# A decoder layer on eight cores: seven-product V projection, a six-row ring in the down projection, and work moved between ScalarE, VectorE and GpSimd

## The chip, the cores and the metric

One Trainium2 chip, all eight cores (two dies: cores 0 to 3 and 4 to 7); each core computes 2048 of 16384 tokens. The metric is the device time of one execution in microseconds (us), that of the slowest core. Some executions of any kernel here fall into a slow state, in which the cores of a die run at a lower granted clock (3339.6 us with die 1 at 0.81 to 0.82, in one execution of the changed kernel; 2976.8 us in one of the kernel before).

Engines: PE is TensorE, DVE is VectorE, ACT is ScalarE, POOL is GpSimd, SP issues transfers.

## The reference, cut to what matters

```python
proj = x @ w_in + b_in                 # x (16384, 2048); columns: qa ka va | qb kb vb
# group A: 8 heads of 128, dilated causal attention, three patterns (window, dilation)
#          (128,1) (512,4) (2048,16), mixed by their softmax denominators
# group B: 16 query heads of 64, 2 key/value heads, sliding window of 128, sinks
# rope on q and k of both groups; RMSNorm of each group; concatenated, @ w_out
x = layer_norm(alpha * x + mixer(x))
x = layer_norm(alpha * x + (silu(x @ w_gate) * (x @ w_up)) @ w_down)      # D_FF = 5632
```

The values va have 1024 columns (A), vb has 128 (B).

## The kernel before

Rope is the rotation of queries and keys by position; PV is the product of the attention weights with V. A core goes through these stages: start (first load, V of token tiles t = 0 and 1), *projection stage* (K of t = 0, then for each tile of 512 tokens V and K, to the first query projection), *sliding-window stage* (32 units u of group B, with query projections in between), *dilated stage* (32 units of group A), out-projection, *MLP stage*, tail (last layer norm). The MLP stage already uses a seven-product (Strassen) scheme: in a down stage a pair p of output rows takes products "1" to "7" in banks BA to BD; `acc` (VectorE) adds a bank into rows `xq` of the residual, which came from memory (x1s in the first half g = 0, the unfinished z2s in the second, g = 1). There are four down stages: two halves of the tokens (st) by two halves of D_FF (g).

```python
# projection stage: V of a block of 128 tokens, plain; B columns in 384-wide groups
groups = [(0, 512), (512, 1024)] if (t < 4 and ...) else [(0, 384), (384, 768), (768, 1152)]
for kc in range(KC):
    matmul(bank(k, bk)[:, 0:c1 - c0], x[:, kc, blk*128:blk*128+128], wv[:, kc, c0:c1], ...)
# K of tile t, head h: 16 matmuls of 512, then a rope of four VectorE operations, then a 128 KB store
# ...
def a_banks(u):                                  # dilated stage: where unit u sums its output
    return (6, 7) if u >= 26 and u % 2 else (OB, LB)
# a unit: 3 scores -> exp on ScalarE -> mask product on VectorE -> PV in a_banks(u)
#         -> a_evac (VectorE reads the bank) -> a_square (ScalarE) -> sum of squares (GpSimd)
# ...
D_OFF = [WB + (24576, 13312, 0)[i] for i in (0, 1, 2, 0, 1, 2, 1, 0)]   # slots of down weights d0..d7
for p in range(8):                               # a down stage
    nxq = load_xq(p + 1)                         # rows of the next pair, five-row ring
    if p == 0:
        for i, bk in (("5", BB), ("2", BC), ("4", BA), ("1", BD)):
            P(i, bk, True, False, range(NJ - 1)) # all but the last h chunk
    ...                                          # the rest of 5, 2, 4, 1, then 3, 7, 6
```

The softmax here doesn't subtract the row's maximum and nothing guards it: scores larger than these inputs give would overflow.

## Time and profile before

| | us |
|---|---|
| executions | 2860.21, 2857.76 fast; 2917.7, 2976.8 slow |
| span of the cores in the profiled execution | 2846.2 to 2858.0, clock 0.99 |
| TensorE busy | 2754.1 (96%) |

Median of the eight cores for each stage, from the starts of the matmuls that open them:

| stage | before, us |
|---|---|
| start | 83.9 |
| projection stage | 417.6 |
| sliding-window stage | 205.7 |
| dilated stage, u = 0 to 25 | 202.1 |
| dilated stage, end: u = 26 to the out-projection | 31.9 |
| out-projection | 230.3 |
| MLP stage | 1649.6 |
| tail | 32.5 |

The lines that show what bounds each of them stand in the prediction. One view is added here, TensorE's timeline of core 7 at the end of the dilated stage; columns are start, duration, engine, line of the kernel, operation, output and input, shape, count, and in brackets the idle time ahead of it with what ended it.

```profile
914.68 0.99 PE L921 MATMUL sp<-arena 128*128 128x128 bf16 x8 [2.25 <-DVE arena L892]
923.98 0.65 PE L947 MATMUL sp<-arena 128*128 128x32 bf16 x17 [0.72 <-DVE arena L900]
929.05 0.65 PE L947 MATMUL sp<-arena 128*128 128x32 bf16 x17 [0.80 <-DVE arena L900]
```

L892 and L900 are VectorE's mask products. After one wait of 2.25 us each unit loses some 0.8 us; the periods of u = 26 to 30, from one unit's first PV matmul to the next, are 6.54, 5.72, 5.01, 5.07 and 5.07 us.

### The profile page before, as it was taken

The numbers are of one execution on the slowest core, as the hardware profiler recorded it, in microseconds if no ns is written. First come the engines' busy times: TensorE is split into PE (matmuls) and PEld (weight loads), VectorE is DVE, ScalarE is ACT, GpSimd is POOL, SyncE is SP. The second block draws the span as 40 slices with busy tenths as digits, with TensorE's granted clock in tenths as the row PEclk, the third lists the DMA queues.
The fourth block names the chain that finished last, engine by engine and source line by source line (L and its number), as shares of the span: only waits on it lengthen the run. The fifth ranks groups of instructions, "written<-read, shape, count | busy, mean of one in ns | idle before, by whom it ended". The sixth has DMA issues, their size and how long they took to land.

```text
span 2858.0 us, 41512 instructions; the slowest of 8 cores (2846.2 to 2858.0 us)
## 1 busy us (share of the span) xinstructions
PE 2754.1 (96%) x15081; PEld 1319.9 (46%) x15081; DVE 1933.6 (68%) x2707; ACT 736.6 (26%) x1078; POOL 562.8 (20%) x569
## 2 busy tenths in 40 slices
PE   6999999999999999999998999988999999999996
PEld 2445555444666444444443444433444444444442
DVE  0654555788788826788865666655888765666667
ACT  0000000576666327333200122111333200212115
POOL 4000000122111567411100000045200000000165
PEclk9999999999999999999999999999999999999998
DMA  9975213668666769799999755699788799555763
GB/s 156 183 138 111 62 52 87 114 98 134 152 138 167 215 144 239 140 151 151 148 159 184 138 89 87 96 199 200 155 175 172 123 196 175 103 89 89 148 133 118
DMA packets 250810, 400.58 MB, mean 140 GB/s; under 512 B 89072, under 2 KB 127088, under 8 KB 249840
## 3 DMA queue, kind: packets, MB, share of 16 engines
q0 software_dynamic: 94272, 186.43, 45.6%
q1 hardware_dynamic: 141936, 182.12, 23.5%
q10 hardware_dynamic: 14400, 29.37, 3.2%
q8 instruction: 122, 2.00, 0.3%
q14 instruction: 80, 0.66, 0.1%
HBM read 491.42 MB, written 97.06 MB: 206 GB/s over the span
## 4 chain that ended last, share of the span: by engine, by line
PE 84%; DMA 7%; DVE 3%; issue 3%; ACT 3%; POOL 1%; DVEq 0%; ACTq 0%; SPq 0%; POOLq 0%
PE sp L1399 49%; PE sp L494 8%; PE sp L1206 8%; PE sp L481 6%; PE sp L742 6%; DMA arena<-wdn 2%; DMA z2s<-arena 1%; DMA arena<-wv 1%; DMA arena<-x1s 1%; DMA arena<-z2s 1%; PE sp L550 1%; ACT arena L791 1%; DVE arena L1745 1%; POOL arena L140 1%; PE sp L514 1%
## 5 line engine op out<-in xcount | busy, mean ns | idle before, releaser
L1399 PE MATMUL sp<-arena 128*128 128x512 f16 x7408 | 1611.0, 380 | 35.7 <-DVE arena L1745 29.8
L1399 PEld LDWEIGHTS sp<-arena 128*128 128x128 f16 (+1 forms) x7408 | 725.3, 98 | 921.7 <-issue 58.0
L1662 DVE TENSOR_TENSOR arena<-sp,arena 128x512 f32<-128x512 f32 (+1 forms) x348 | 236.5, 688 | 160.7 <-PE sp L1399 145.3
L1745 DVE TENSOR_TENSOR arena<-arena,sp 128x512 f32<-128x512 f32 x257 | 167.8, 682 | 135.9 <-PE sp L1399 122.7
L742 PE MATMUL sp<-arena 128*128 128x512 bf16 x1024 | 237.0, 380 | 3.8 <-DVE arena L375 1.5
L1206 PE MATMUL sp<-arena 128*128 128x512 bf16 x1024 | 221.8, 379 | 1.0 <-DVE arena L1195 1.0
L494 PE MATMUL sp<-arena 128*128 128x512 bf16 x1024 | 222.2, 379 | 0.0
L140 POOL DMA_DIRECT2D arena<-wup x88 | 65.7, 747 | 782.1 <-DVE arena L1412 501.0
L463 DVE TENSOR_TENSOR arena<-sp,arena 128x384 bf16<-128x384 f32 (+1 forms) x81 | 48.1, 605 | 203.0 <-PE sp L481 120.0
L481 PE MATMUL sp<-arena 128*128 128x384 bf16 (+1 forms) x1040 | 182.6, 337 | 0.0
L1412 DVE TENSOR_TENSOR arena<-arena 128x2048 f16<-128x2048 bf16 (+1 forms) x118 | 158.9, 1347 | 30.7 <-DMA arena<-wdn 30.7
L1249 POOL TENSOR_TENSOR arena<-arena 128x512 f32<-128x512 f32 x117 | 150.3, 1285 | 145.1 <-DVE arena L1745 107.5
L1696 ACT ACTIVATE arena<-sp 128x512 f32<-128x512 f32 x86 | 51.4, 597 | 436.4 <-PE sp L1399 436.4
L1420 DVE TENSOR_TENSOR arena<-arena 128x2048 f16<-128x2048 bf16 (+1 forms) x118 | 159.3, 1350 | 0.0
L1251 POOL TENSOR_TENSOR arena<-arena 128x512 f32<-128x512 f32 x117 | 156.7, 1340 | 10.4 <-ACT arena L1248 8.0
L1206 PEld LDWEIGHTS sp<-arena 128*128 128x128 bf16 x1024 | 100.0, 98 | 122.9 <-issue 3.2
L1662 DVE TENSOR_TENSOR arena<-arena 128x512 f16<-128x512 f32 (+1 forms) x304 | 155.0, 568 | 2.4 <-DMA x1h<-arena 2.4
L494 PEld LDWEIGHTS sp<-arena 128*128 128x128 bf16 x1024 | 100.2, 98 | 120.3
L369 ACT ACTIVATE arena<-sp,arena 128x512 bf16<-128x512 f32 (+1 forms) x37 | 24.7, 666 | 506.1 <-PE sp L514 430.8
L1248 ACT ACTIVATE arena<-arena 128x512 f32<-128x512 f32 x117 | 73.7, 630 | 311.2 <-DVE arena L1745 160.4
L742 PEld LDWEIGHTS sp<-arena 128*128 128x128 bf16 x1024 | 95.9, 98 | 123.2 <-issue 14.8
L481 PEld LDWEIGHTS sp<-arena 128*128 128x128 bf16 x1040 | 101.7, 98 | 79.6
(145 smaller groups left out, 2493.1 us busy)
## 6 DMA issues: line engine op xcount, KB each, us to landing
arena<-wup POOLq DMA_DIRECT2D x88, 1024.0 KB, 10.8
arena<-wdn POOLq DMA_DIRECT2D x32, 1408.0 KB, 19.0
z2s<-arena SPq DMA_DIRECT2D x48, 512.0 KB, 11.9
arena<-wob SPq DMA_DIRECT2D x32, 512.0 KB, 7.2
arena<-xres SPq DMA_DIRECT2D x32, 512.0 KB, 8.7
x1s<-arena ACTq DMA_DIRECT2D x64, 256.0 KB, 8.8
arena<-x1s SPq DMA_DIRECT2D x32, 512.0 KB, 13.5
arena<-z2s SPq DMA_DIRECT2D x32, 512.0 KB, 15.6
```

The lines of the kernel that those rows point to most:

```text
L140: i = self._add(q, lambda: eng.dma_start(out=out, in_=in_), reads, writes, joins, semkey=semkey)
L481: ins = nc.tensor.matmul(bank(k, bk)[:, 0:c1 - c0], x[:, kc, blk * 128:blk * 128 + 128], wv[:, kc, c0:c1], start=(kc == 0), stop=(kc == KC ...
L494: ins = nc.tensor.matmul(bank(k, bk), wk[h][:, kc, :], x[:, kc, :], start=(kc == 0), stop=(kc == KC - 1))
L742: ins = nc.tensor.matmul(bank(k, bk), w[:, kc, :], x[:, kc, :], start=(kc == 0), stop=(kc == KC - 1))
L1206: ins = nc.tensor.matmul(bank(k, bk), w[:, kc, :], y[:, kc, hh * 512:(hh + 1) * 512], start=(first and i == 0), stop=(last and i == len(kc ...
L1249: S_.pool(lambda: nc.gpsimd.tensor_tensor(out=za, in0=za, in1=z, op=ALU.add), [bz, bza], [bza])
L1251: ss["pend"] = [lambda: S_.pool(lambda: nc.gpsimd.tensor_tensor(out=qa, in0=qa, in1=sq, op=ALU.add), [bsq, bqa], [bqa])]
L1399: ins = nc.tensor.matmul(bank(k, bk), w, x, start=(first and i == 0), stop=(last and i == len(ws) - 1), skip_group_check=True)
L1412: S_.dve(lambda: nc.vector.tensor_tensor(out=v, in0=w[:, 0:n, :], in1=w[:, n:2 * n, :], op=ALU.add), [bw], [b])
L1420: S_.dve(lambda: nc.vector.tensor_tensor(out=v, in0=w[:, :, 0:128], in1=w[:, :, 128:256], op=ALU.subtract), [bw], [b])
L1662: S_.dve(lambda: nc.vector.tensor_tensor(out=o, in0=a, in1=b, op=op), [ba, bb], [bo])
L1745: S_.dve(lambda: nc.vector.tensor_tensor(out=v, in0=v, in1=o, op=op), [b, bo], [b])
```

## The change

Its intent: fewer matmuls in V (a seven-product scheme for the 1024 A columns of t = 2 to 7), and no waits for weights and rows in the down stages. To find room for V's sums one of the five x slots is given up, and another holds two rope tables until x of t = 7 needs it. The rest moves small work from VectorE to ScalarE or from ScalarE to GpSimd. The core of the diff, with cuts:

```diff
+    if swap:                                   # rope_a: the half swap as two ScalarE copies, one VectorE product
+        for i, j in ((0, 64), (64, 0)):
+            S_.act(lambda i=i, j=j: nc.scalar.activation(out=t2[i:i + 64], in_=ps[j:j + 64], func=AF.Identity, ...
-    xs = [view(k, XO + i * X_SLOT, ...) for i in range(5)]
+    xs = [view(k, XO + i * X_SLOT, ...) for i in range(4)]
-    def v_tile(t, blk): ...
+    def w_sum(i): ...      # five sums of blocks of wv (128x4096), once
+    def x_sum(t, i): ...   # three sums of blocks of x for each tile
+    def v_unit(t, i, mid=None): ...   # products 4 5 1 2 3 7 6, eight matmuls of 512 each, for 256 tokens
+    def vb_tile(t): ...    # B columns: 64 matmuls of 128 columns
-    load_ra(0)
+    load_ta(0)
+    load_ta(1)             # second rope table, ahead of V of t = 1
 ...
-        return (6, 7) if u >= 26 and u % 2 else (OB, LB)
+        return (6, 7) if u >= 28 and u % 2 else (OB, LB)
 ...
-            S_.act(lambda: nc.scalar.activation(out=sq, in_=yc, func=AF.Square), [byc], [SQ[1]])
+            if 26 <= 4 * h + c < 31:
+                S_.pool(lambda: nc.gpsimd.tensor_tensor(out=sq, in0=yc, in1=yc, op=ALU.mult), [byc], [SQ[1]])
+            else:
+                S_.act(lambda: nc.scalar.activation(out=sq, in_=yc, func=AF.Square), [byc], [SQ[1]])
 ...                          # sliding-window stage: dilated q ropes one step later, three with swap on ScalarE;
                              # dilated stage: run(dveq, 2 if u < 27 else 4), before u < 26
-        proj(u + LEAD, mid=lambda: run(peq, 1))
         run(dveq, 4)
+        proj(u + LEAD, mid=(lambda: run(peq, 1)) if u < 31 else first_a)
 ...
-D_OFF = [WB + (24576, 13312, 0)[i] for i in (0, 1, 2, 0, 1, 2, 1, 0)]
+D_OFF = [WB + (13312, 24576, 0)[p % 3] for p in range(8)]
 ...                          # down stages: six-row ring, rows of pair p + 2 asked for in the middle of pair p
+                e = (3, 4, 5, 2, 0, 1)[n % 6]
-                nxq = load_xq(p + 1) if p < 7 else None
+                    if p < 6:
+                        load_xq(p + 2)
 ...                          # first pair: product 2 whole, ahead of the last h chunk
+                        P(i, bk, True, i == "2", None if i == "2" else range(NJ - 1))
 ...                          # x1h of the other half of the tokens: in halves, over seven pairs
-                    if 1 <= p <= 4:
-                        load_x1((B11, B22, B12, B21)[p - 1])
+                    for i in {6: (6, 7), 7: ()}.get(p, (p,)):
+                        load_x1(i)
```

## The prediction

> **What bounds the kernel now.** I read the list of cores first, then the page's first part. The eight cores lie within 2846 to 2858 us at a granted clock of 0.99, so any of them may stand for all; the third timed run (2917.7) is the slow state, and the fast time is 2859 (2857.8 and 2860.2).
>
> ```profile
> PE 2754.1 (96%) x15081; PEld 1319.9 (46%) x15081; DVE 1933.6 (68%) x2707; ACT 736.6 (26%) x1078; POOL 562.8 (20%) x569
> ```
>
> TensorE is busy for 96% of the span. So time can go in two ways only: fewer matmuls, or less of the 2858 - 2754 = 104 us in which TensorE idles. Some 22 us of that lie in the first load of x and wv, and 27 us behind the last matmuls (VectorE and ScalarE finish the layer norm there); the change touches neither. About 55 us are in reach. Next, the groups of instructions kept apart by shape, for what the matmuls cost:
>
> ```profile
> L494 PE MATMUL sp<-arena 128*128 128x512 bf16 x1024 | 222.2, 379 | 0.0
> L481 PE MATMUL sp<-arena 128*128 128x384 bf16 x816 | 134.1, 326 | 0.0
> L481 PE MATMUL sp<-arena 128*128 128x512 bf16 x224 | 48.7, 379 | 0.0
> L872 PE MATMUL sp<-arena 128*128 128x128 bf16 x256 | 21.5, 228 | 0.0
> L921 PE MATMUL sp<-arena 128*128 128x128 bf16 x256 | 19.9, 222 | 2.8 <-DVE arena L892 2.3 <-DVE arena L851 0.6
> ```
>
> L494 is K's projection, L481 V's. Ahead of the bar stand busy us over the count (the mean ns after it is latency, which overlaps): 222.2/1024 = 0.217 us for a 512-column matmul, 134.1/816 = 0.164 for 384, but 0.078 to 0.084 for 128, dearer than a quarter of 0.217. The idle column of L494 and L481 is 0.0: in the projection stage TensorE never waits once it runs. The idle time I looked for in TensorE's timeline over the two down-projection stages of the first half (st 0):
>
> ```profile
> 1453.99 2.53 PE L1399 MATMUL sp<-arena 128*128 128x512 f16 x11 [0.96 <-DVE arena L1743]
> 1456.71 47.64 PE L1399 MATMUL sp<-arena 128*128 128x512 f16 x220 [0.20 <-DVE arena L1745]
> 1506.66 2.53 PE L1399 MATMUL sp<-arena 128*128 128x512 f16 x11 [2.30 <-DVE arena L1743]
> 1510.92 33.40 PE L1399 MATMUL sp<-arena 128*128 128x512 f16 x154 [1.73 <-DVE arena L1745]
> 1547.22 16.78 PE L1399 MATMUL sp<-arena 128*128 128x512 f16 x77 [2.90 <-DVE arena L1745]
> 1565.66 296.93 PE L1399 MATMUL sp<-arena 128*128 128x512 f16 x1375 [1.66 <-DVE arena L1745]
> ...
> 1920.94 37.80 PE L1399 MATMUL sp<-arena 128*128 128x512 f16 x165 [7.01 <-DVE arena L1745]
> 1967.08 47.90 PE L1399 MATMUL sp<-arena 128*128 128x512 f16 x208 [8.34 <-DVE arena L1745]
> ```
>
> TensorE waits for a PSUM bank that VectorE has not emptied. VectorE takes its work in order, so I looked at what it stood behind (its timeline, same stretch):
>
> ```profile
> 1505.82 0.69 DVE L1743 SCALAR_TENSOR_TENSOR arena<-arena,sp 128x512 f32<-128x512 f32 x1 [6.10 <-DMA arena<-x1s]
> 1544.85 1.62 DVE L1412 TENSOR_TENSOR arena<-arena 128x2816 f16<-128x2816 bf16 x1 [6.43 <-DMA arena<-wdn]
> ...
> 1920.11 0.69 DVE L1745 TENSOR_TENSOR arena<-arena,sp 128x512 f32<-128x512 f32 x1 [7.85 <-DMA arena<-z2s]
> 1964.71 1.63 DVE L1412 TENSOR_TENSOR arena<-arena 128x2816 f16<-128x2816 bf16 x1 [10.92 <-DMA arena<-wdn]
> ```
>
> So the root is DMA: rows of the residual (x1s, z2s) and down weights (wdn) that land late. By their place, the wdn waits are always those of the pairs p = 6 and 7.
>
> **What the Trainium skill says.** "TensorE: Matmul & The Clock Gate", section "Back-to-back issue gap", gives about 81 ns for a 128-column matmul that follows its own weight load; the trace agrees (78 to 84). Its 131 ns for 512 columns does not fit: the trace has 217, which is the same section's isolated figure, 216. Section "What's actually happening" of that page: after an idle window of about 3.4 us the clock falls to half and comes back only after as long a busy one. The trace agrees: behind the 8.34 us idle, 208 matmuls took 47.90 us against 208 x 0.216 = 44.9. "DMA: Bandwidth & Descriptors", section "Queues, rings and completion order": an engine serves its queues in turn, a packet at a time, so a small store shares with a wide load. The trace: a 128 KB K store lands in 1.9 to 2.3 us when no x load is under way (176 to 196 us) and in 7 to 12 us when one is. "VectorE: DVE Perf Modes", section "Side-by-side: where the cycles go for N=2048 bf16", gives 1224 ns in the doubled mode that a tensor_tensor of 16-bit data can reach; the trace has 1240 for the 2048-element sums.
>
> **The change, part by part.**
> *1. Strassen V.* For t = 2..7 the 1024 A columns take 7 products of 8 matmuls per 128+128 tokens: 6 x 2 x 56 = 672 matmuls of 512, instead of 768 equivalents. The B columns, before part of the 384-wide groups, become 16 + 4 x 64 = 272 matmuls of 128 columns. Removed: 134.1 + 48.7 = 182.8 us. Added: 672 x 0.217 = 145.8, and 272 x 0.080 = 21.8 (estimate from L872 and L921). Net -15.2, all on the path, as TensorE never waits here. A third of the Strassen gain goes into the narrow matmuls.
> VectorE: K's rope loses two 0.75 half operations for one 0.69 product on 64 tiles, -52 us, with ScalarE (idle here) taking two copies of about 0.6 each. It gains 9 x 0.69 for each of 12 units (75), 6.1 of x sums for each of 6 tiles (37; 1.24 per 2048 elements), 12 of weight sums and 3 of B columns, minus the old 48: net +27 us over 400. It has 33 us of work in 63 now, so on the average it stays hidden. One place does not: x sums for t = 2 stand inside K of t = 1, at about 127 us, and x2's second half landed at 129.7 (issued at 31.1, 98.6 to landing). By my hand schedule VectorE then ends that K stage at 149.6, while the sixth product of the first V unit wants a bank at 147.7: +3. Net of part 1: -12.
> *2. Queries.* In the sliding-window stage the steady period (5.6 us) is a loop of ScalarE operations and one VectorE product, so moving t1 ahead buys nothing there. At its end the dilated q ropes hold VectorE (2.93 us of TensorE idle at 682.7, 0.58 and 1.38 at 706 and 710; clock 0.96 in 682 to 725): ropes deferred by one step and three swaps on ScalarE, -3. At the end of the dilated stage (6.3 us idle, clock 0.95 in 910 to 942) ScalarE is full; five squares of 0.62 moved to GpSimd, -3.
> *3. Down stages.* Idle there sums, over four stages, to: first pair 4 x (0.96 + 0.20) = 4.6; weights of pairs 6 and 7: 2.90 + 1.66 + 8.34 + 2.48 + 2.44 = 17.8; rows: 2.30 + 1.73 + 7.01 + 0.52 = 11.6. All 34.0. The weight slots now rotate by three, so d6 can start when pair 3 is done, not pair 4: a pair (16.6 us) earlier, against waits of at most 10.9: I take 16 back. The sixth ring row lets pair p+2's rows start in the middle of pair p, some 10 us more lead against waits up to 7.9; I take 8 of 11.6, as transfers are crowded. Product 2 of the first pair, which needs only finished h blocks, now runs whole before the last chunk: 4 of 4.6. With the waits, the cold clock behind the long ones goes (2.2 and 3.0 us): 4. Sum -32.
> *4. Entry to the query stage.* Its weights and tables now go where wv and the x sums lay, so they load in K of t = 7 (27.6 us) instead of long before: +1.
> Sum: -12 - 6 - 32 + 1 = -49 us; 2859 - 49 = 2810.
>
> **The rivals.**
> *The transfers are the bound of the down stages.* In the table of stretches for the z2s stage:
>
> ```profile
> 1880.00:1897.00 17.00, 17.00 (x81) 7.69 (x79) 9.97 (x13) 1.96 (x4) 10.18 (x9) 1.00 1.01 210
> 1914.00:1931.00 17.00, 10.06 (x38) 4.14 (x39) 9.54 (x12) 1.29 (x3) 5.73 (x5) 0.80 0.94 250
> 1965.00:1982.00 17.00, 14.92 (x56) 6.22 (x57) 10.26 (x14) 2.52 (x4) 11.26 (x9) 0.77 1.01 180
> ```
>
> The last two columns are the DMA share (1.01: all 16 engines busy) and GB/s. The same bytes in fewer us need a higher rate, and then the waits come back under new names. Against it: the stretch before (1820 to 1845) has 0.72 and the one after (2016 to 2033) 0.58, earlier loads can use the first, and x1h is cut in halves and spread over seven pairs. If it holds, part 3 gives 14 and the time is 2828.
> *VectorE or a late x holds V.* Each V unit wants nine VectorE products (6.2 us) in 12.1 us of matmuls, and an in-order queue behind one late transfer stops all of them; only four x slots remain. Against it: x(t+3) starts some 90 us before its first use, and x7 has 37 us for two transfers of about 8. If it holds in every tile, part 1 is eaten: 2822.
> *Everything lands.* All of parts 1 and 3 and the clock come back, and 8 us in part 2: 2798.
>
> **Range and chances.** Part 1 is matmul counting and sure to some 4 us; part 3 has the spread, 14 to 39. The range is 2795 to 2832. The line for 2% faster is 0.98 x 2859 = 2802; reaching it needs nearly all of part 3, 0.29. Within 2%: 0.69. Slower by 2% needs a new wait in every tile: 0.02.
>
> **What would show it right or wrong.** TensorE's busy time should fall by 15 to 22 us, with 672 matmuls of 512 and 272 of 128 in V at 0.217 and 0.08. At 127 us VectorE should wait for x2, once. The idle in front of the down matmuls should fall from 34 to about 6, with no wait for wdn and what is left in the z2s stage. The projection stage should end some 12 us earlier than 501. I am wrong if the 128-column matmuls cost over 0.1, if V units show idle for x, rope tables or stores, if the query stage begins with a wait for its weights, or if the DMA share in the down stages stays at 1.0 with as much idle as now.

## The result, and the profile after

The changed kernel is correct. Its fast executions are 2822.86, 2821.32, 2820.68 and 2816.33 us. The ratio to the kernel before is 0.9865, 95% interval 0.9841 to 0.9888: 1.35% faster, where the prediction's 2810 over 2859 meant 1.7%. (Ratios are the mean time of one kernel's fast runs over that of the other's fast runs of the same rounds, so not quite the ratio of the medians quoted.) Two executions were slow (3339.62 and 2945.26).

| stage, median of eight cores | before | after | change | predicted |
|---|---|---|---|---|
| start | 83.9 | 84.7 | +0.7 | 0 |
| projection stage | 417.6 | 404.8 | -12.8 | -11 (parts 1 and 4) |
| sliding-window stage | 205.7 | 205.65 | -0.06 | -3, with the next row |
| dilated stage, u = 0 to 25 | 202.1 | 200.7 | -1.45 | |
| dilated stage, end | 31.9 | 38.1 | **+6.2** | -3 |
| out-projection | 230.3 | 230.3 | 0.0 | 0 |
| MLP stage | 1649.6 | 1617.6 | -32.0 | -32 |
| tail | 32.5 | 31.8 | -0.7 | 0 |

One row has the wrong sign: 9 of the 10 us by which the prediction was off lie in the 38 us of the dilated stage's end. The first part of the page of the changed kernel:

```profile
PE 2729.1 (97%) x14985; PEld 1299.9 (46%) x14985; DVE 1949.5 (69%) x2711; ACT 833.5 (30%) x1219; POOL 573.8 (20%) x574
```

TensorE's busy time fell by 25 (the prediction had 15 to 22), VectorE's rose by 16, ScalarE's by 97. The groups that replace V's (L537 the products, L581 the narrow B columns; L1054 is the dilated stage's PV, L921 before), busy us and mean latency behind the bar, then idle:

```profile
L537 PE MATMUL sp<-arena 128*128 128x512 f16 x480 | 111.7, 385 | 5.6 <-ACT arena L553 5.6
L537 PE MATMUL sp<-arena 128*128 128x512 bf16 x192 | 45.4, 379 | 0.0
...
L1054 PE MATMUL sp<-arena 128*128 128x128 bf16 x256 | 19.9, 222 | 6.3 <-DVE arena L1108 4.7 <-DVE arena L1025 1.6
...
L581 PE MATMUL sp<-arena 128*128 128x128 bf16 x272 | 16.0, 219 | 0.0
```

L581: 16.0/272 = 0.059 us for a matmul of 128 columns, not the 0.080 I took from L872 and L921. Both are the same matmul. L1054 comes in groups of eight: 256 matmuls are 32 groups, 19.9/32 = 0.62 us each, and 7 steps of 0.056 from start to start (the trace has 0.055 to 0.057 in L1054 and L581 alike) plus one latency of 0.222 make 0.61. The busy time of a short group contains the latency of its last matmul; 64 in a row hide it. So busy time over count is an issue rate only in long runs.

In TensorE's timeline V of t = 2 has one stall, and VectorE's timeline shows what it was behind (L488 writes V of t = 1, L358 ends a K rope):

```profile
153.03 12.30 PE L537 MATMUL sp<-arena 128*128 128x512 f16 x45 [5.55 <-ACT arena L553]
```

```profile
93.64 1.29 DVE L488 TENSOR_TENSOR arena<-sp,arena 128x512 bf16<-128x512 f32 x2 [12.61 <-DMA vs<-arena]
97.54 1.29 DVE L488 TENSOR_TENSOR arena<-sp,arena 128x512 bf16<-128x512 f32 x2 [2.61 <-DMA vs<-arena]
...
133.24 0.69 DVE L358 TENSOR_TENSOR arena<-arena 128x512 bf16<-128x512 f32 x1 [2.81 <-DMA ka<-arena]
...
141.43 0.69 DVE L358 TENSOR_TENSOR arena<-arena 128x512 bf16<-128x512 f32 x1 [1.91 <-DMA ka<-arena]
```

VectorE never waits for x2 here; it waits for V stores and K stores to free their buffers. The granted clock is 0.50 from 151.1 to 157.9 us, behind TensorE's idle time. Two V stores of this stretch took 17.2 and 16.3 us (issued 76.33 and 81.10), 10.9 and 11.3 in the kernel before; two rope tables of 512 KB had just been asked for (68.05 and 68.80), before only one. The end of the dilated stage, and the down stages, in TensorE's timeline:

```profile
902.96 0.61 PE L1054 MATMUL sp<-arena 128*128 128x128 bf16 x8 [2.21 <-DVE arena L1108]
905.18 0.87 PE L1005 MATMUL sp<-arena 128*128 128x128 bf16 x8 [1.18 <-DVE arena L358]
912.71 1.01 PE L1054 MATMUL sp<-arena 128*128 128x128 bf16 x8 [2.50 <-DVE arena L1108]
```

```profile
1930.50 2.53 PE L1547 MATMUL sp<-arena 128*128 128x512 f16 x11 [2.55 <-DVE arena L1903]
1934.76 14.40 PE L1547 MATMUL sp<-arena 128*128 128x512 f16 x66 [1.73 <-DVE arena L1903]
1950.26 2.53 PE L1547 MATMUL sp<-arena 128*128 128x512 f16 x11 [1.09 <-DVE arena L1903]
1954.53 21.53 PE L1547 MATMUL sp<-arena 128*128 128x512 f16 x99 [1.73 <-DVE arena L1903]
1981.63 9.95 PE L1547 MATMUL sp<-arena 128*128 128x512 f16 x32 [5.58 <-DMA arena<-x1h]
```

L1108 is a_evac, VectorE's reading of a finished unit's bank: TensorE waits for the bank, twice. In the down stages (L1547, before L1399) the waits for wdn are gone; what is left lies in one stage (st 0, g = 1) and is a wait for rows of z2s, passed on by VectorE (L1903), and a new one for x1h. The idle time in front of L1547 is 0.0 to 12.7 us by core, 23.4 to 38.9 before.

### The profile page after: what moved, and what is told of

Same layout as the page of the kernel before. It is cut to its first block, busy times and chain, and to the rows that moved or that the text cites. A ratio compares the mean times of both kernels' runs of the same rounds, so it can differ in the third digit from the quotient of the medians.

```text
span 2821.7 us, 41756 instructions; the slowest of 8 cores (2803.3 to 2821.7 us)
## 1 busy us (share of the span) xinstructions
PE 2729.1 (97%) x14985; PEld 1299.9 (46%) x14985; DVE 1949.5 (69%) x2711; ACT 833.5 (30%) x1219; POOL 573.8 (20%) x574
## 4 chain that ended last, share of the span: by engine, by line
PE 82%; DMA 7%; DVE 5%; ACT 3%; issue 2%; POOL 1%; SPq 0%; DVEq 0%; ACTq 0%; POOLq 0%
PE sp L1547 52%; PE sp L1353 8%; PE sp L601 6%; PE sp L537 5%; PE sp L874 5%; DMA z2s<-arena 3%; ACT arena L924 2%; DMA vs<-arena 1%; DMA arena<-wv 1%; DVE arena L984 1%; DMA ka<-arena 1%; DMA arena<-x1h 1%; POOL arena L140 1%; PE sp L1005 1%; PE sp L581 1%
## 5 line engine op out<-in xcount | busy, mean ns | idle before, releaser
L1547 PE MATMUL sp<-arena 128*128 128x512 f16 x7408 | 1603.4, 379 | 12.7 <-DVE arena L1903 7.1
L1547 PEld LDWEIGHTS sp<-arena 128*128 128x128 f16 (+1 forms) x7408 | 725.1, 98 | 891.4 <-issue 21.3
L1903 DVE TENSOR_TENSOR arena<-arena,sp 128x512 f32<-128x512 f32 x257 | 169.7, 682 | 154.9 <-PE sp L1547 135.4
L874 PE MATMUL sp<-arena 128*128 128x512 bf16 x1024 | 236.7, 379 | 2.5 <-DVE arena L355 2.5
L362 ACT ACTIVATE arena<-sp,arena 64x512 f32<-64x512 f32 x134 | 91.5, 683 | 288.3 <-PE sp L601 248.9
L1854 ACT ACTIVATE arena<-sp 128x512 f32<-128x512 f32 x86 | 51.4, 597 | 416.9 <-PE sp L1547 416.9
L1353 PEld LDWEIGHTS sp<-arena 128*128 128x128 bf16 x1024 | 100.0, 98 | 122.9 <-issue 3.2
L537 PE MATMUL sp<-arena 128*128 128x512 f16 (+1 forms) x672 | 150.1, 383 | 5.6 <-ACT arena L553 5.6
L601 PEld LDWEIGHTS sp<-arena 128*128 128x128 bf16 x1024 | 100.0, 98 | 119.6
L874 PEld LDWEIGHTS sp<-arena 128*128 128x128 bf16 x1024 | 95.5, 98 | 120.1 <-issue 11.4
L1817 ACT ACTIVATE arena<-sp 128x512 f32<-128x512 f32 x90 | 53.5, 597 | 278.9 <-PE sp L1547 256.0
L1022 ACT ACTIVATE arena<-sp 128x1024 bf16<-128x1024 f32 x96 | 97.6, 1020 | 78.7 <-PE sp L1016 59.5
## 6 DMA issues: line engine op xcount, KB each, us to landing
arena<-z2s SPq DMA_DIRECT2D x29, 512.0 KB, 12.7
```

What stands on the lines that cost most here:

```text
L537: ins = nc.tensor.matmul(bank(k, bk), w[:, c, :], m[:, c, :], start=(first and c == 0), stop=(last and c == 7), skip_group_check=True)
L601: ins = nc.tensor.matmul(bank(k, bk), wk[h][:, kc, :], x[:, kc, :], start=(kc == 0), stop=(kc == KC - 1))
L874: ins = nc.tensor.matmul(bank(k, bk), w[:, kc, :], x[:, kc, :], start=(kc == 0), stop=(kc == KC - 1))
L1022: S_.act(lambda: nc.scalar.activation(out=p, in_=sp[:, :], func=AF.Exp, scale=scA), spb[s], [bp])
L1353: ins = nc.tensor.matmul(bank(k, bk), w[:, kc, :], y[:, kc, hh * 512:(hh + 1) * 512], start=(first and i == 0), stop=(last and i == len(kc ...
L1547: ins = nc.tensor.matmul(bank(k, bk), w, x, start=(first and i == 0), stop=(last and i == len(ws) - 1), skip_group_check=True)
```

## The experiments

Each is the changed kernel with the edit shown. Where no timing is given, one execution was profiled and the stages were read on all eight cores; the medians of stages that an edit does not touch repeat to 0.2 us in the sliding-window stage and in the first 26 dilated units. They lie between 37.0 and 38.1 at the end of the dilated stage (38.1, the highest, in the first profile; 37.5 on the average of the nine others), between 1611 and 1622 in the MLP stage and, for the unedited projection stage, between 400 and 403 (404.8 in the first profile). Of the kernel before there is one profile only. All results are correct but the one marked.

**Banks put back.**

```diff
-        return (6, 7) if u >= 28 and u % 2 else (OB, LB)
+        return (6, 7) if u >= 26 and u % 2 else (OB, LB)
```

> Only the bank choice of the dilated stage is put back: odd units take banks 6 and 7 from u = 26 on, as in the kernel before, not from 28. Measured so far, median of the eight cores: the end of the dilated stage (units 26 to 31, to the first matmul of the out-projection) 31.9 us before, 38.1 after. Bank theory: unit 27 waits for the bank that unit 26's evacuation holds (2.21 and 2.50 us in the chain ahead of units 27 and 28 on core 7); the stage comes to 33 to 35 us and unit 26's period from 9.75 to about 6.5. GpSimd theory (squares on GpSimd stretch the VectorE operations beside them): the stage stays above 37 us.

End of the dilated stage: 35.8 us (38.1 in the first profile, 37.5 on the average). The period of 9.75 on core 7, which is unit 27's (my text numbers it 26), fell to 6.12 (4.9 to 6.4 by core), and unit 26's rose from 6.50 to 7.15. The bank theory holds for some 2 us, not for all.

**Squares put back.**

```diff
-            if 26 <= 4 * h + c < 31:
+            if False:
```

> Only the five squares of the dilated stage's end go back from GpSimd to ScalarE. GpSimd theory: the VectorE operations that took 1.7 us beside a square (0.65 to 0.68 without) are short again, units 28 to 30 go from 5.5 to 5.7 us back to about 5.1, and the end of the dilated stage goes from 38.1 to 36 us or less. Bank theory: unit 26's period stays near 9.7 us and the stage above 36. My prediction's step (ScalarE is full, so the squares gain 3 us on GpSimd): the stage gets 3 us longer, 41.

35.1 us: 3.0 less than the first profile, 2.4 less than the average. Unit 30 has a period of 5.07 us again (5.72), while unit 27's stays long, 8.4 to 9.7 by core, as the bank theory has it. My step that GpSimd gains 3 us has the wrong sign.

**Both put back.**

> Both undone together. If banks and squares are the whole of what was lost at the end of the dilated stage, it comes to 32 us or less, as in the kernel before (31.9); if something else (a rope of the last queries, the out-projection's weights) has a share, it stays at 34 or more.

33.0 us: 5.2 of the 6.2 lost by the first profile, 4.5 of 5.6 by the average; units 28 to 30 take 5.01, 5.07 and 5.07. About 1 us remains (0.7 in the two combined runs below). Unit 26's period is 7.15 on every core, 6.54 before: unit 27's first PV matmul waits 2.87 us for L355, the third operation of a query rope (core 7, at 896.31). In the kernel before this operation ran ahead of the mask product L892 (912.04 and 913.84 us); now it stands behind L1025, L1028 and L1108 (893.05 to 895.42). That points to another one-line edit, `run(dveq, 2 if u < 27 else 4)`, where the bound was 26. No run undoes it, so this is not shown.

How five small squares cost 3 us shows in the timelines of the run with only the banks put back. GpSimd, then VectorE, the same stretch on core 7:

```profile
908.99 1.26 POOL L1125 TENSOR_TENSOR arena<-arena 128x512 f32<-128x512 bf16 x1 [6.43 <-DVE arena L1108]
910.39 1.64 POOL L1131 TENSOR_TENSOR arena<-arena 128x512 f32<-128x512 f32 x1
```

```profile
909.45 0.84 DVE L1033 TENSOR_TENSOR arena<-arena 128x64 bf16<-128x64 bf16 x1
910.22 0.68 DVE L1025 TENSOR_TENSOR arena<-arena 128x1024 bf16<-128x1024 bf16 x1
910.82 1.75 DVE L1028 TENSOR_TENSOR arena<-arena 128x1024 bf16<-128x1024 bf16 x1
```

And VectorE in the run with both put back:

```profile
905.67 0.19 DVE L1033 TENSOR_TENSOR arena<-arena 128x64 bf16<-128x64 bf16 x1
905.78 0.69 DVE L1025 TENSOR_TENSOR arena<-arena 128x1024 bf16<-128x1024 bf16 x1
906.87 1.28 DVE L1028 TENSOR_TENSOR arena<-arena 128x1024 bf16<-128x1024 bf16 x1 [0.40 <-ACT arena L1022]
```

L1033, 64 columns, takes 0.84 us beside the square and ends at 910.29, just when the square does (910.25); L1028 starts at 910.82 and ends at 912.57, 0.54 us behind the end of GpSimd's sum (912.03). VectorE seems to stand still until GpSimd's instruction is over. (The other way round too: the sum takes 1.64 us here, begun while L1025 ran, and 1.27 in the run below at 905.60 us, where hardly any VectorE work overlaps it. GpSimd's spans are rough in this profile; the argument rests on VectorE's own times.) In the second run the 0.19 is back, L1028 loses 0.6 to the sum alone, and the bracket shows VectorE waiting for ScalarE again (0.40); in the first, from 906.8 us on, it goes from one operation to the next without a gap. There VectorE is the bound. The Trainium skill says it: "SBUF — State Buffer", section "SBUF: two separate sides", has one pair of ports shared by GpSimd and VectorE, an exclusive lock for the whole instruction, taken by GpSimd or by a VectorE operation in a two-port mode or with two SBUF inputs, and "the other fully blocks". The trace agrees, with the numbers above. I had not looked it up. Whether the block or the slow square itself costs the time, the next run tells.

**Squares nobody waits for.** Both put back, and five squares more on GpSimd, whose result is unused.

```diff
                 S_.pool(... out=ac, in0=ac, in1=sq, op=ALU.add ...)
+                if 26 <= 4 * h + c < 31:
+                    S_.pool(lambda: nc.gpsimd.tensor_tensor(out=sq, in0=yc, in1=yc, op=ALU.mult), [byc], [SQ[1]])
```

> Banks and squares as in the kernel before (end of the dilated stage 33.0 us alone), and five squares more on GpSimd, behind its sums, whose result nobody uses. Block theory (VectorE stands still while GpSimd works): VectorE's 1024-wide products beside it take 1.7 us again and the stage goes to 35 us or more. Latency theory (the squares were slow and their users waited): nobody waits here, so the stage stays at 33 within 0.5 us.

35.7 us: 2.8 more than without them, as much as the real squares (35.8 against 33.0). The first line is VectorE with both put back; then GpSimd and VectorE of this run, core 7 (L1342 and L1344 are the same two normalising products, ahead of the out-projection):

```profile
913.14 1.40 DVE L1342 SCALAR_TENSOR_TENSOR arena<-arena 128x512 bf16<-128x512 bf16 x2
```

```profile
913.26 1.30 POOL L1133 TENSOR_TENSOR arena<-arena 128x512 f32<-128x512 bf16 x1
```

```profile
913.59 2.19 DVE L1344 SCALAR_TENSOR_TENSOR arena<-arena 128x512 bf16<-128x512 bf16 x2
```

Beside the unused square the pair takes 2.19 us, 0.79 more, and the periods of u = 29 and 30 grow by as much, from 5.07 to 5.85. No engine's wait in this stretch names GpSimd. It is the block, not the latency. (It fell on other operations than I had expected: the 1024-wide product beside the sum takes 1.35 to 1.40 us here, and 1.28 to 1.33 without the unused squares.)

**The second rope table later.**

```diff
     load_ta(0)
-    load_ta(1)
     ...                     # V of t = 1
+    load_ta(1)
     load_x(2, (8, 8))
```

> The load of the second rope table (512 KB) moves from right after V of t = 0 to just before the load of x for t = 2, so that one table, not two, stands beside the V stores of t = 1. Those took 16 to 17 us to land (11 in the kernel before), K's ropes of t = 1 began some 7 us later, and V of t = 2 took 32.3 us where the later tiles take 24.2. Table theory: V stores land in about 11 us again and V of t = 2 comes to 24 to 27 us, the projection stage from 404.8 to about 398. Rival (my prediction's step: x2 itself, or the K stores, hold VectorE): V of t = 2 stays above 29 us.

V of t = 2 takes 25.6 us (median; 32.2 in the first profile, but 29.3 on the average of the eleven other runs that leave this alone, so 4 us is the fair gain of this run; the combined run below, with the same edit, has 27.5, which would be 2), the projection stage 398.5, and V stores of this stretch land in about 11.5 us again (11.7 and 11.1 on core 0). The table theory holds for a part of the stall, 2 to 4 us. On core 7, K stores still hold VectorE for 2.76, 2.31 and 2.35 us.

**x2 first.**

```diff
+    load_x(2, (8, 8))       # ahead of the B-column weights, at the start
     ...
-    load_x(2, (8, 8))       # behind V of t = 1
```

> x for t = 2 is requested at the start, ahead of the B-column weights, some 85 us sooner. My prediction's step said that x2's lateness costs V of t = 2 its stall. If so, V of t = 2 goes from 32 (29 on average in the last runs) to 25 us or less. Rival (the V stores behind two rope tables make VectorE late, x2 was there in time): with x2 out of the way of the K stores (2.81 and 1.91 us of VectorE waits for those) it gains at most 3 us, and V of t = 2 stays above 27; the start may get longer by up to 3 us, as the B-column weights come behind it.

V of t = 2 takes 30.1 us, no less. x2's lateness, which I had named, is not the cause. The start did not get longer (82.5).

**Query ropes without ScalarE.**

```diff
-                   swap=tau in (33, 35, 37))
+                   swap=False)
```

> Only the three query ropes whose half swaps went to ScalarE (at the end of the sliding-window stage) go back to VectorE alone. Measured: sliding-window stage, to the first dilated PV, 205.7 us before and 205.65 after, where I had predicted -3; two waits of TensorE for those ropes (1.17 and 1.36 us) stand in the chain of core 7. Theory A (the swap on ScalarE sends the rope through two engines and makes it later): the stage gets 1 to 2.5 us shorter, 203 to 204.6. Theory B (my prediction's: VectorE is the crowded one, the swaps help): it gets 1 to 3 us longer. Rival C (neither engine sets the end there, the loop of ScalarE operations does): within 0.4 us.

204.0 us in the sliding-window stage (and 204.0 and 204.1 in the two combined runs), 1.6 less: as theory A forecast. In the changed kernel the stage ends with these waits on core 7 (L874 is the query projection, which wants the bank that L355, the rope's first read on VectorE, has not left):

```profile
671.16 3.61 PE L874 MATMUL sp<-arena 128*128 128x512 bf16 x16 [1.17 <-DVE arena L355]
...
683.27 3.61 PE L874 MATMUL sp<-arena 128*128 128x512 bf16 x16 [1.36 <-DVE arena L355]
```

With the swap a bank is read by two engines, and comes free when the second is done; that this is why the rope is later is my reading, not tested further. The undone version has four such waits, of 0.44 to 1.17 us, and still ends earlier.

**The order of the deferred ropes put back.**

```diff
-        run(dveq, 4)
         proj(u + LEAD, ...)
+        run(dveq, 4)
```

> Only the order of one step: the deferred rope operations are again issued after the query projection, as in the kernel before. If deferring them is what gave the shorter period of unit 27 (8.27 to 5.10 us) the sliding-window stage goes from 205.65 to 207 or more; if the later ropes are what costs 1.2 us at units 28 and 30 (6.54 each), it goes to 204.5 or less; a change within 0.4 us says that it moves the wait and not the end.

207.4 us, and the first 26 dilated units take 202.9 instead of 200.7: the deferral is worth 1.8 + 2.2 = 4.0 us. So the -3 that I gave to this end was there, and the swaps on ScalarE took 1.6 of it back. Of the two, I had counted both as gains.

**d6's slot put back.**

```diff
-D_OFF = [WB + (13312, 24576, 0)[p % 3] for p in range(8)]
+D_OFF = [WB + (13312, 24576, 0)[i] for i in (0, 1, 2, 0, 1, 2, 1, 0)]
```

> Only the slot order of the down weights is put back, so that d6 waits for pair 4 again and not for pair 3. My prediction's step: this order is worth 16 us over the four down stages. If so, the MLP stage goes from 1617.6 us (median of the first profile of the changed kernel; 1613 to 1622 in seven later runs that do not touch it) to 1628 or more, with wdn waits of 2 to 10 us ahead of VectorE for pairs 6 and 7. Rival (once rows and x1h are spread, the transfers are early enough whatever the slot): within 4 us.

The MLP stage takes 1624.5 us: 7 above 1617.6, and only 3 above the highest of the runs that leave it alone. On core 2, VectorE waits for wdn four times, 7.63, 12.91, 4.73 and 1.82 us, on core 6 four times, 14.3 us in all; it waits for no z2s row on either. The idle time in front of the down matmuls is 18.4 us on core 2, but 2.4 on core 6. So much of VectorE's wait for wdn comes back (27 and 29 us on these cores in the kernel before), but TensorE stands still for a part of it only; the size is 7, not 16.

**The first pair put back.** Product 2 again takes its last chunk behind the others, and the rest of the pair follows the old order.

```diff
-                        P(i, bk, True, i == "2", None if i == "2" else range(NJ - 1))
+                        P(i, bk, True, False, range(NJ - 1))
```

> Only the first pair of each down stage goes back to its old order (all four first products wait for the last h chunk), with slots and ring as changed. My prediction's step: 4 us over four stages (waits of 0.96 and 0.20 us in each). If so, these two waits are back and the MLP stage is 3 to 5 us longer. Rival: the weight sums and rows now come earlier and the wait is hidden: under 1 us.

1617.9 us: no loss in the median, but the spread of that median would hide one. The waits are back on every core, 0.96 and 0.20 us in each of the four stages, 4.6 us, which is what I had summed. The three quietest cores (0, 3 and 6) have no other and take 1615.2, where the quietest of the changed kernel take 1609.0, so there the gain is real. On the other cores 2 to 13 us of waits for z2s rows, x1h and the like come on top, 0 to 13 in the changed kernel. That a gain ahead of the z2s stage is in part lost again there, where transfers set the end, is my reading and not shown.

**The ring with five rows.** Rows of p + 1 are asked for at the start of pair p, as before; slots and first pair as changed. The fourth down stage does not use the ring and is left alone. The sixth row and the earlier request are undone together; which of them gains is not separated.

```diff
-                e = (3, 4, 5, 2, 0, 1)[n % 6]
+                e = (3, 4, 0, 1, 2)[n % 5] if not last else (3, 4, 5, 2, 0, 1)[n % 6]
-                    load_xq(p + 2)           # in the middle of pair p
+                    load_xq(p + 1)           # at the start of pair p
```

> Only the sixth row of the ring is not used: rows of pair p+1 are requested at the start of pair p, as in the kernel before, not those of p+2 in its middle; slots and first pair as changed. My prediction's step: the ring is worth 8 us of rows (x1s, z2s). If so, the MLP stage is 6 to 12 us longer, with waits for x1s and z2s of 2 to 7 us ahead of VectorE. Rival (DMA-bound: rows come no sooner for being asked for sooner): within 3 us.

1645.4 us: 28 more, nearly the whole gain of part 3. VectorE's groups on core 0 (L1903 adds a bank to a row, L1901 is the first time a row is touched), and the first of them in the changed kernel (core 7), with idle time and what ended it behind the last bar:

```profile
L1903 DVE TENSOR_TENSOR arena<-arena,sp 128x512 f32<-128x512 f32 x257 | 168.2, 682 | 147.4 <-PE sp L1547 100.1 <-DMA arena<-z2s 47.0 <-DVE arena L1903 0.2
L1901 DVE SCALAR_TENSOR_TENSOR arena<-arena,sp 128x512 f32<-128x512 f32 x64 | 43.2, 684 | 74.8 <-DMA arena<-x1s 50.3 <-PE sp L1547 24.6
```

```profile
L1903 DVE TENSOR_TENSOR arena<-arena,sp 128x512 f32<-128x512 f32 x257 | 169.7, 682 | 154.9 <-PE sp L1547 135.4 <-DMA arena<-z2s 19.3 <-DVE arena L1903 0.2
```

With five rows VectorE waits 97 us for rows (z2s and x1s; 93 on core 7), with six 19 for z2s alone. No wait for wdn comes back (30.7 us of VectorE's time on core 7 of the kernel before, none on cores 0 and 7 here), but there it had waited only 45 us for rows: rows take the place of weights.

**x1h earlier.**

```diff
-                    for i in {6: (6, 7), 7: ()}.get(p, (p,)):
+                    for i in {4: (4, 5), 5: (6, 7), 6: (), 7: ()}.get(p, (p,)):
```

> The last four half loads of x1h in the z2s stage are requested one and two pairs sooner. Measured: one wait of TensorE for x1h of 1.3 to 5.6 us, by core, behind the last pair. Lateness theory (asked for too late): that wait is gone, the MLP stage is 2 to 4 us shorter (1617.6 in the first profile, 1613 to 1622 in the last four) and no wait ahead of it grows by more than 1 us. Rival (the transfers are the bound there, DMA share 1.0): the wait for z2s rows or weights grows by as much, and the stage stays within 2 us.

1618.1 us, no gain that the spread would show: no wait for x1h is left on the cores looked at, but the waits for z2s rows grew, in sum from 5.1 to 7.4 us on core 0 and from 7.1 to 8.6 on core 7. That fits the rival, and the next run tests it.

**A quarter of x1h's bytes.** The result is wrong (relative error 0.116).

```diff
-        S_.dma("act", xall[:, b, h:h + 4, :], k.x1h_d[b, :, h:h + 4], ...
+        S_.dma("act", xall[:, b, h:h + 1, :], k.x1h_d[b, :, h:h + 1], ...
```

> The changed kernel with only a quarter of the bytes of each x1h load; the result is wrong on purpose. If the transfers bound what is left of the idle time in the z2s stage, both the wait for x1h and those for z2s rows go, and all cores come to the floor of the MLP stage, 1609 us (median 1617.6 with all bytes). If the rows are late for another reason (asked for late, behind stores in their queue), z2s waits of 3 us or more stay and the median stays above 1613.

1609.5 us, seven cores at 1609.0 to 1611.0 and one at 1614.4. The stretch of 136 us over the z2s stage on core 7, changed kernel and then this run; after the engines' busy times come the granted clock, the DMA share and GB/s:

```profile
1857.00:1993.00 136.00, 123.31 (x552) 54.71 (x551) 78.93 (x91) 17.67 (x28) 77.05 (x64) 0.97 0.99 217
```

```profile
1857.00:1993.00 136.00, 132.50 (x605) 59.57 (x604) 88.74 (x103) 24.21 (x37) 78.01 (x66) 1.00 0.95 196
```

All 16 DMA engines are busy for 0.99 of the stretch; with fewer bytes TensorE runs 9 us more of it. So most of the idle time left there is set by the transfers.

**The four gains together.** Banks, squares, table and query ropes, timed in five rounds.

> The four edits that gained by themselves together: banks 6 and 7 from u = 26, squares on ScalarE, the second rope table behind V of t = 1, query ropes without ScalarE. Measured alone by stage: 5.2 us together for the first two (38.1 to 33.0), 3 to 6 for the table (V of t = 2), 1.6 for the ropes. If they add up, 10 to 13 us: about 2810 against 2822, a ratio to the kernel before of 0.981 to 0.984. Rival (one of them only moves a wait that then stands elsewhere): 0.985 or more.

Fast runs 2803.5 to 2812.9 us (one of six was slow), ratio to the kernel before 0.9824 (0.9810 to 0.9839), against 0.9865 of the changed kernel. It beats both. Stages: projection 400.3, sliding-window 204.0, end of the dilated stage 32.6, MLP 1611.7 (untouched; within its spread). V of t = 2 is 24.0 to 30.3 us by core.

**The table later still.** As the last, but the table is asked for in K of t = 0, after its sixth head.

> The four gains together, with the second rope table asked for in K of t = 0 after its sixth head, not right behind V of t = 1. If the table beside K's first stores is what still held V of t = 2 at 24 to 30 us (median 27.5), V of t = 2 comes to 24 to 25.5 on all cores and the time to some 2 us less than 2809. Rival (the stores wait for one another or for x2): V of t = 2 stays at 27 to 28.

V of t = 2: 25.6 to 28.7 us, median 26.4; ratio 0.9832 (0.9809 to 0.9856), no better. The first wait for a K store shrinks (core 0: 3.61 to 1.20 us), but VectorE now waits for the table itself, 3.70 to 7.16 us at 126 to 131 us. The store's wait turned into the table's. On core 0 VectorE also waits 1.20 us for x2, at 131 us: the wait that I had predicted shows once the others shrink.

## Why the prediction was right or wrong

**The step that failed is part 2's second half:** "At the end of the dilated stage ... ScalarE is full; five squares of 0.62 moved to GpSimd, -3." It came to +6.2 in the first profile, +5.6 on the average of the runs that leave it alone. Two things stand in its place. The squares cost 2.4 to 3.0 us (and five unused ones 2.8): I asked how long a square takes on the engine that gets it, and not whom it stops; VectorE, which that step leaves out, became the bound of the units, with periods of 5.7 instead of 5.07. And I left a one-line edit out of the sum, the bank threshold: some 2 us, as unit 27 now waits for the bank of unit 26. About 1 us is open; the trace points to a second one-line edit that I had left out, the bound of `run(dveq, ...)`.

**Part 2's first half** (-3) came to -1.5 over the sliding-window stage and the first 26 dilated units: the deferral gave 4.0, the swaps took 1.6 back, the rest is open.

**Part 1** (-12, with +1 of part 4; -12.8 measured) was right in its sum by luck, as two errors cancelled. The narrow matmuls cost 0.059, not 0.080, 21.8 - 16.0 = 6 us less, from the misread busy time. That is what the B columns had cost before (182.8 - 768 x 0.217 = 16.1), so no part of the Strassen gain went into them; the "third" of my text is a quarter by its own numbers (5.7 of 20.9). The stall at t = 2 was of 5.6 us of idle time where I had +3, and some 8 with the halved clock behind it: V of t = 2 took 32.2, the quietest core of any run 24.0. On the average of the eleven other runs it took 29.3, and the projection stage 402.2, which is -15.4. Its cause was not the late x2: moving x2 changes nothing, moving a rope table gives 2 to 4; waits for K stores remain. From t = 3 on no V unit waits; that rival is ruled out. Part 4's wait for the query weights did not show: the query projection's only waits (2.5 us) are the two shown.

**Part 3** (-32, and -32.0 measured, with a spread of 11 between single profiles) was right in its sum, again by luck, and wrong in its terms. I had given 16 to the slots, 8 to the ring and 4 to the first pair, by what ended each wait in the kernel before. Undone alone they cost 7, 28 and 0 (4.6 on quiet cores). The sum of 35 is within the spread of 32, so whether they add is not shown. The shares were wrong because the last wait was taken for the cause: with the slots changed and the ring not, the waits for weights become waits for rows, and TensorE idles 28 us there (30 before). The prediction's first rival, waits that come back under new names, is true of the slots without the ring, and of what is left in the z2s stage, though not of the whole. The new x1h wait was not foreseen.

## What to carry to other kernels

Before moving work to an idle engine, ask what it shares with the engine that is nearly full, not only how long it takes there. When a stage is fed by several transfers, the name at the end of a wait is the last to land and not the share of the gain: undo each part alone. Take the issue rate of a matmul from a long run, and subtract one latency for each short group. Read a stage in several runs that leave it alone before taking a difference of one or two us for the effect of an edit.

## What the Trainium skill lacked or had wrong

- "TensorE: Matmul & The Clock Gate", section "Back-to-back issue gap": about 81 ns for each 128-column matmul in a stream of weight load and matmul. 64 in a row, each with its own load, ran at 0.059 us (272 in 16.0 us; 0.056 from start to start), near the 56 ns that the page gives as the isolated figure. For 512 columns it has 131; the trace has 0.217 us throughout. At both widths the isolated figure fits and the sustained one does not. The agreement with 81 that my prediction claimed was an artefact of short groups.
- "SBUF — State Buffer", section "SBUF: two separate sides": right. It gives no size for arithmetic on both engines: here five squares of 1.26 us on GpSimd, each followed by a sum of 1.64, beside VectorE products of 0.19 and 0.68 us, lengthened these to 0.84 and 1.75 and the stage by 2.4 to 3 us.
